# Spreading the first norm with one ones product, and a new order for the first stage, in a one-layer diffusion trunk on one core

## The chip, the core and the metric

The kernel runs on one core of a Trainium2 chip. The core has a matrix engine (TensorE, PE in the profile, with its weight loads listed apart as PEld), VectorE (DVE), ScalarE (ACT), GpSimd (POOL), and queues that issue DMAs (SyncE's is SPq, ScalarE's is ACTq). Each engine runs its own instructions in order and waits on semaphores for the others. The metric is the device time of one execution in microseconds (us), the median of several.

## The reference

One layer of a flow-matching backbone. 1024 latent tokens `x` and 256 context tokens `ctx` of width 1024 go through a feed-forward half step, a token mixing of retention and gated linear attention, and a second feed-forward half step; each is modulated by columns that a condition vector gives. What matters here is the beginning:

```python
cond_lat = jax.nn.silu(c)
m_l = jnp.split(cond_lat @ ada_w[i] + ada_b[i], N_MOD, axis=-1)
x = x + 0.5 * m_l[2][:, None, :] * swiglu(modulate(rms_norm(x, norm1_w[i]), m_l[0], m_l[1]),
                                            ffn1_w1[i], ffn1_w3[i], ffn1_w2[i])

def rms_norm(x, w):
    y = xf * lax.rsqrt(jnp.mean(xf * xf, axis=-1, keepdims=True) + EPS)
def modulate(h, shift, scale):
    return h * (1.0 + scale[:, None, :]) + shift[:, None, :]
def swiglu(h, w1, w3, w2):
    return (jax.nn.silu(h @ w1) * (h @ w3)) @ w2
```

The norm of 1024 tokens needs the sum of squares over the width; scale and shift need products of the condition with 1024 x 1024 blocks of `ada_w`; then come the products with `w1` and `w3`.

## The kernel before

**Layout.** Activations stand with the width on the 128 partitions and tokens along the row: `x` is eight tiles (k = 0 to 7) of 128 x 512 for each of two token groups, 0 and 1. A float product is made of three faster ones: each operand is split in a high part, rounded by ScalarE (`hh`, `wh`, `whi`), and a low part, the rest, made by VectorE (`hl`, `wl`, `wlo`), and TensorE adds up high x high, high x low and low x high. Both parts of four k tiles of one weight chunk come from one 128 x 512 half, `raw`.

**The first stages** (`first1`, L1139 to L1303) do the norm of group 0, its first columns, and the products of six weight chunks i = 0 to 5 (alternating `w1` and `w3`) with the eight k tiles. The order on TensorE, VectorE and ScalarE is the order in which the lines are written, since the call stands in a `manual_schedule` for these three. SyncE's queue follows the order of the text as far as buffers and the limited number of DMAs under way allow.

- `squares` (L547) makes the sum of squares: ScalarE squares a tile, VectorE adds it to `nacc`.
- `rstd_col` (L559) sums `nacc` over the partitions by four products with ones that give columns, and forms power -0.5 of the mean (`pow_half`, L1596): one VectorE step and one on GpSimd. `rows_diag` (L570) multiplies the identity with each column, and `rstd_rows` (L575) spreads the diagonals over all partitions with four more products. The result stands in PSUM (`pr`) and is copied to `rb[0]` (`nrb`).
- A modulation column j (8 and 9 are the scales of k = 0 and 1, 0 and 1 the shifts) can be had in two ways. `pe_load` fetches 512 KB, `pe_sums` (L470) makes partial sums in 16 products on TensorE, ScalarE copies these out of PSUM, `pe_turn` (L481) turns them into a column with a small product, and `pe_out` (L485) adds the bias on ScalarE; `mod_fin` (L526) finishes a scale on VectorE. Or `mod_load` fetches 512 KB and `mod_sum` (L501) sums on VectorE against the condition row that `cond_load` and `cond_silu` (L442, L452) make; scales 10 to 15 go this way.
- The condition's own columns `ccol` come laid out from the host, and `pe_cond` (L457) puts them through Silu.
- `norm_a1` (L599, VectorE) forms the normed and scaled tile, `norm_a2` (L602, ScalarE) adds the shift and rounds it to `hh`, `norm_b` (L605, VectorE) makes `hl`. `norm_a` does the first two.
- `fetch` loads a raw half, `high` and `low` make its two parts, `load` does both. `mms(i, k, js)` issues the products j of weight i with tile k: 0 is high x high, 1 needs `hl`, 2 needs the weight's low part. `warm` issues filler products.

Stage 0 is k = 0, written out by hand (L1190 to L1245). The loop at L1246 has stages st = 1 to 7. In each, behind weight 0's products, come the sums and the scale of tile n = st + 1, and behind weight 2's its shift, `hh` and `hl`, then the second halves of weights (`FIRST`) and the squares of token group 1 (`SQ`, with loads `X1`). Stage 7 has Silu and products of the hidden values, weights 6 and 7 and the second norm instead.

Later phases (the rest of the feed-forward net, the mixing and the second net) use the same primitives; some follow a planner. Between phases the x tiles are read again (L2025).

Of the kernel before, what the change touches and what calls it, by code (L numbers as in the profile page):

```python
# [11 lines left out]
F32 = mybir.dt.float32  # L12
# [378 lines left out]
class Trunk:  # L391
# [36 lines left out]
    def consts(self):  # L428
# [3 lines left out]
        self.pad(cp, 16)  # L432
        self.ident = self.tile(cp, [P, P], F32, "ident")
        nc.scalar.dma_start(self.ident, I["ident"])
# [3 lines left out]
        nc.vector.memset(self.mhalf, -0.5)  # L438
        self.mods = self.tile(cp, [P, 112], F32, "mod")
# [17 lines left out]
    def pe_cond(self, pool):  # L457
        nc = self.nc
        t = self.tile(pool, [P, 36 * KD], F32, "ccol")[:, :33 * KD]
        nc.scalar.dma_start(t, self.I["ccol"])  # L460
        self.sel = t[:, 32 * KD:32 * KD + 2]
        self.ccol = t[:, :32 * KD]
        nc.scalar.activation(self.ccol, self.ccol, AF.Silu)
# [675 lines left out]
    def first1(self, pools, n1):  # L1139
# [28 lines left out]
        def products(i, ks):  # L1168
            for k in ks:
                self.mm3(pss[i], self.wslice(ws[i], k), self.h[0][k], k == 0, k == KD - 1)  # L1170

# [4 lines left out]
        def mms(i, k, js):  # L1176
            w, h = self.wslice(ws[i], k), self.h[0][k]
            for j in js:
                u, v = ((0, 0), (0, 1), (1, 0))[j]
                nc.tensor.matmul(pss[i], w[u], h[v], start=k == 0 and j == 0, stop=k == KD - 1 and j == js[-1])  # L1180
# [7 lines left out]
        x0, x1 = self.x[0], None  # L1188
        self.ndg, idle, pss, acc = 4, self.psA(), {}, None
# [16 lines left out]
        low(0, 0, raw)  # L1206
        self.rstd_rows(n1r, 512, n1, dg=dg, pr=pr)
        raw = high(1, 0)
        self.pe_sums(pc, 0, cur[9])
        warm(WARM[2])  # L1210
        self.norm_a(0, 0, a, b, pr, n1, x0[0])
        rb[0] = self.scr(n1, "nrb")
        nc.scalar.copy(rb[0], pr)
        low(1, 0, raw)
        sm = self.pe_copy(pc, P, n1)
        self.norm_b(0, 0, b, x0[0])
        for i in range(2):
            pss[i] = self.psA()
            mms(i, 0, (0, 2))
        o9 = self.pe_turn(rc, 4, sm[0])  # L1220
        for i in range(2):
            mms(i, 0, (1,))
        load(2, 0)
        self.pe_out(9, o9)
        load(3, 0)
        self.norm_a1(0, 1, a, rb[0], x0[1])
        self.pe_sums(pc, P, cur[1])
        raw = high(4, 0)
        sm = self.tile(n1, [P, P], F32, "csum128", 2)
        nc.scalar.copy(sm, pc[:, P:2 * P])  # L1230
        low(4, 0, raw)
        load(5, 0)
        cur = {}
# [3 lines left out]
        for i in range(2, 6):  # L1237
            if i == 4:
                o1 = self.pe_turn(rc, 6, sm)
                self.pe_out(1, o1)  # L1240
                self.norm_a2(0, 1, b, x0[1])
            pss[i] = (self.psA if i < 4 else self.psB)()
            mms(i, 0, (0, 2, 1))
        self.norm_b(0, 1, b, x0[1])
        self.cond_silu()  # L1245
        for st in range(1, KD):  # L1246
            n = st + 1
            for w in FIRST.get(st, ()):
                fetch(*w)
            if st in X1:  # L1250
                self.load_x(pools, (1,), X1[st])
            if n + 2 < KD:
                cur[10 + n], cur[n + 2] = self.mod_load(10 + n), self.pe_load(n + 2)
# [3 lines left out]
            for i in range(6):  # L1257
                mms(i, st, (0, 2, 1))
                if i == 0 and n < KD:
# [3 lines left out]
                if i == 2 and n < KD:  # L1263
# [7 lines left out]
                if n == KD:  # L1271
# [682 lines left out]
    def run(self):  # L1954
# [18 lines left out]
        warm = self.tile(self.dp, [P, 64], F32, "warm")[:, :8]  # L1973
        nc.scalar.activation(warm, self.mhalf, AF.Silu)
# [48 lines left out]
        for at, (tg, k) in zip(xat, ((tg, 4 * q + k) for tg, q in ((0, 0), (1, 1), (0, 1), (1, 0)) for k in range(4))):  # L2023
            o = TGS[tg][0]
            plan[at].append(lambda tg=tg, k=k, o=o: nc.sync.dma_start(self.x[tg][k], I["xT"][k * P:(k + 1) * P, o:o + 512]))  # L2025
# [204 lines left out]
for _n, _w in (("ada_b", 72), ("norm1_w", 8), ("norm2_w", 8), ("norm3_w", 8), ("final_norm_w", 8),  # L2230
               ("ret_norm_w", 4), ("gla_norm_w", 4), ("gla_b", 4)):
# [9 lines left out]
def layout(inputs):  # L2241
# [3 lines left out]
    A["xT"] = c(g["x"][0].T)  # L2245
# [5 lines left out]
    A["ccol"] = np.zeros((P, 33 * KD), np.float32)  # L2251
    for i, n in enumerate(("c", "c_ctx")):
        A["ccol"][:, i:32 * KD:32] = g[n].reshape(KD, P).T
        A["ccol"][i::32, 32 * KD + i] = 1.0
# [69 lines left out]
```

## Time and profile before

| what | value |
|---|---|
| median of 3 runs | 2091.38 us (2090.43 to 2091.49) |
| the profiled execution's own time | 2092.0 us |
| its span, first to last instruction | 2090.2 us |
| VectorE, ScalarE, GpSimd busy | 70%, 46%, 9% of the span |
| TensorE's granted clock, mean | 0.999 |
| DMA, mean | 175 GB/s |

A row of the timeline gives start, length, engine, line of the code, operation, `out<-in` by tile names, count, and in brackets the idle time of the engine ahead of it with what ended it. A float product on TensorE is two records. Weight loads run beside products.

### The profile page before, as it was taken

What the parts mean: (1) busy time and instruction counts of PE and PEld (TensorE: products, weight loads), DVE (VectorE), ACT (ScalarE), POOL (GpSimd) and SP (SyncE); (2) the same over time, 40 slices, a digit from 0 to 9 for tenths busy, and PEclk for the clock granted to TensorE, in tenths of its full rate; (3) what the DMA queues carried; (4) which work ended last, traced back from release to release, by engine and by line L of the source; (5) the groups of instructions that cost most, each with busy time, mean ns of one, the idle gap of its engine ahead of it and who ended that gap; (6) DMA issues with size and microseconds to landing.
All of it is one profiled execution on the core that took longest, in us unless ns stands there. A gap on an engine that the chain in (4) does not pass through costs nothing.

```text
span 2090.2 us, 34659 instructions
## 1 busy us (share of the span) xinstructions
PE 2075.5 (99%) x12646; PEld 1780.3 (85%) x12646; DVE 1463.5 (70%) x2649; ACT 965.9 (46%) x1806; POOL 198.2 (9%) x196
## 2 busy tenths in 40 slices
PE   9999999999999999999999999999999999999998
PEld 7888888888889999899789988888888888888888
DVE  6889999676775445764687368867776666765676
ACT  5433433435544445564664246444434334334553
POOL 0000000000015664001011001000000000010000
PEclk9999999999999999999999999999999999999999
DMA  9267767459886553673322223342344444477674
GB/s 347 86 236 235 238 219 255 151 168 353 294 290 219 181 185 105 197 217 93 89 76 84 78 75 102 101 161 81 109 159 146 144 164 156 151 240 232 218 228 151
DMA packets 199643, 366.54 MB, mean 175 GB/s; under 512 B 23216, under 2 KB 36400, under 8 KB 199472
## 3 DMA queue, kind: packets, MB, share of 16 engines
q1 hardware_dynamic: 199040, 364.07, 52.4%
q8 instruction: 99, 1.62, 0.3%
q14 instruction: 72, 0.59, 0.1%
q10 hardware_dynamic: 432, 0.26, 0.0%
HBM read 289.66 MB, written 66.19 MB: 170 GB/s over the span
## 4 chain that ended last, share of the span: by engine, by line
PE 89%; DMA 5%; DVE 4%; ACT 1%; issue 1%; SPq 0%; DVEq 0%; POOL 0%; POOLq 0%; ACTq 0%
PE psa L147 17%; PE psa L424 12%; PE psa L426 12%; PE psa L425 12%; PE psb L425 9%; PE psb L426 8%; PE psb L424 8%; PE psb L147 8%; DMA hh<-in_w 1%; DMA raw<-in_w 1%; PE psa L1180 1%; DMA raw<-gd 1%; DVE wlo L420 1%; DVE hl L420 1%; DVE nacc L556 1%
## 5 line engine op out<-in xcount | busy, mean ns | idle before, releaser
L419 ACT ACTIVATE whi<-raw 128x512 fp32r<-128x512 f32 x371 | 233.9, 631 | 498.0 <-issue 160.1
L420 DVE TENSOR_TENSOR wlo<-raw,whi 128x512 fp32r<-128x512 f32 x371 | 254.5, 687 | 176.1 <-ACT whi L419 172.6
L424 PE MATMUL psa<-hh,whi 128*128 128x512 f32 x684 | 266.8, 390 | 0.0
L426 PE MATMUL psa<-hh,wlo 128*128 128x512 f32 x684 | 266.2, 389 | 0.0
L425 PE MATMUL psa<-hl,whi 128*128 128x512 f32 x684 | 266.1, 389 | 0.0
L425 PE MATMUL psb<-hl,whi 128*128 128x512 f32 x568 | 221.3, 390 | 1.0 <-DVE hl L420 0.9
L424 PE MATMUL psb<-hh,whi 128*128 128x512 f32 x568 | 221.1, 389 | 0.0
L426 PE MATMUL psb<-hh,wlo 128*128 128x512 f32 x568 | 221.1, 389 | 0.0
L147 PE MATMUL psa<-hl,whi 128*128 128x512 f32 x384 | 153.1, 399 | 0.0
L147 PE MATMUL psa<-hh,whi 128*128 128x512 f32 x384 | 152.3, 397 | 0.0
L147 PE MATMUL psa<-hh,wlo 128*128 128x512 f32 x384 | 152.0, 396 | 0.0
L424 PEld LDWEIGHTS psa<-hh,whi 128*128 128x128 f32 x684 | 128.4, 188 | 27.2 <-ACT s L693 0.5
L426 PEld LDWEIGHTS psa<-hh,wlo 128*128 128x128 f32 x684 | 128.3, 188 | 26.6 <-DVE wlo L420 0.2
L425 PEld LDWEIGHTS psa<-hl,whi 128*128 128x128 f32 x684 | 128.4, 188 | 26.4
L147 DVE TENSOR_TENSOR wlo<-raw,whi 128x512 fp32r<-128x512 f32 (+1 forms) x132 | 82.8, 643 | 94.0 <-ACT whi L147 90.0
L420 POOL TENSOR_TENSOR hl<-s,hh 128x512 fp32r<-128x512 f32 x88 | 131.8, 1524 | 145.7 <-ACT hh L419 140.5
L147 ACT ACTIVATE whi<-raw 128x512 fp32r<-128x512 f32 (+1 forms) x132 | 77.2, 598 | 119.9 <-PE psa L147 100.6
L425 PEld LDWEIGHTS psb<-hl,whi 128*128 128x128 f32 x568 | 106.6, 188 | 24.3 <-DVE hl L420 2.1
L424 PEld LDWEIGHTS psb<-hh,whi 128*128 128x128 f32 x568 | 106.6, 188 | 22.6 <-ACT hh L419 0.4
L426 PEld LDWEIGHTS psb<-hh,wlo 128*128 128x128 f32 x568 | 106.6, 188 | 22.1 <-DVE wlo L420 0.2
L426 PE MATMUL psa<-hh,hl 128*128 128x256 f32 x392 | 111.1, 283 | 0.0
L424 PE MATMUL psa<-hh,hh 128*128 128x256 f32 x392 | 111.1, 283 | 0.0
(414 smaller groups left out, 4910.9 us busy)
## 6 DMA issues: line engine op xcount, KB each, us to landing
raw<-in_w SPq DMA_DIRECT2D x242, 256.0 KB, 3.3
s<-in_w SPq DMA_DIRECT2D x198, 256.0 KB, 3.9
gd<-s SPq DMA_DIRECT2D x154, 256.0 KB, 2.8
ada<-in_adaT SPq DMA_DIRECT2D x60, 512.0 KB, 4.4
raw<-gd SPq DMA_DIRECT2D x91, 256.0 KB, 3.2
sd<-s SPq DMA_DIRECT2D x44, 256.0 KB, 2.7
raw<-sd SPq DMA_DIRECT2D x44, 256.0 KB, 3.0
hh<-in_w SPq DMA_DIRECT2D x44, 256.0 KB, 4.1
```

The source lines that it names most:

```text
L147: self.rec.add(self.eng, lambda: f(*map(get, a), **{x: get(v) for x, v in k.items()}), outs, ins, name, a, k)
L419: nc.scalar.activation(hi, src, AF.Copy)
L420: (eng or nc.vector).tensor_tensor(out=lo, in0=src, in1=hi.bitcast(F32), op=ALU.subtract)
L424: mm(ps, wa[0], xa[0], start=start, stop=False, skip_group_check=more)
L425: mm(ps, wa[0], xa[1], start=False, stop=False, skip_group_check=more)
L426: mm(ps, wa[1], xa[0], start=False, stop=stop, skip_group_check=more)
L556: nc.vector.tensor_tensor(out=acc[:, :n], in0=acc[:, :n], in1=sq[:, :n], op=ALU.add)
L1180: nc.tensor.matmul(pss[i], w[u], h[v], start=k == 0 and j == 0, stop=k == KD - 1 and j == js[-1])
```

## The change

Eight edits, all but the last two in or for the first stages:

1. The norm of group 0 is spread by one product of ones with the whole of `nacc` (all partitions get the sum), then a logarithm with the bias `eps` and scale 1/D and an exponential with scale -0.5, both on ScalarE, give `rb[0]`. The columns, GpSimd's power, the diagonals and their products go. The table set with both functions is loaded at the start, in place of Silu's.
2. VectorE copies the sums of columns 8, 0 and 9 out of PSUM and puts out these columns (`pe_out` with `dve=True`), ahead of the low parts of weights.
3. The condition's columns come with `cols`, 16 numbers a partition, and Silu is made of an exponential on ScalarE and an add, a reciprocal and a product on VectorE, into a zeroed `ccol`. `ccol`'s own load goes, and the identity's moves from ScalarE's queue to the end of SyncE's first loads. On that queue the halves of weights 2 and 3 move ahead of column 9's load, and those of 4 and 5 ahead of column 1's.
4. Products of stage 0 are in a new order, and column 9's sums come behind the first four of them. Filler products: 30 and 8 for 40, 2 and 4.
5. In stage 1 the scale and shift of tile 2 come behind weights 2 and 3, not 0 and 2. The condition row is loaded behind stage 0's products.
6. The squares of group 1 are spread as 3, 2 and 3 over stages 4 to 6 (were 4, 2, 2), its loads come behind the columns' loads, and in stage 7 its column sum comes behind weight 3.
7. `xT` is stored by the host as two blocks of 1024 x 512, so that a tile is one contiguous piece of memory, here and where x is read again.
8. Padding and constants are moved accordingly.

```diff
-        self.pad(cp, 16)
+        self.pad(cp, 20)
         self.ident = self.tile(cp, [P, P], F32, "ident")
-        nc.scalar.dma_start(self.ident, I["ident"])
+        self.eps = self.tile(cp, [P, 8], F32, "eps")
+        nc.vector.memset(self.eps, EPS)
...
     def pe_cond(self, pool):
         nc = self.nc
-        t = self.tile(pool, [P, 36 * KD], F32, "ccol")[:, :33 * KD]
-        nc.scalar.dma_start(t, self.I["ccol"])
-        self.sel = t[:, 32 * KD:32 * KD + 2]
-        self.ccol = t[:, :32 * KD]
-        nc.scalar.activation(self.ccol, self.ccol, AF.Silu)
+        self.sel = self.col("sel")
+        self.ccol = self.tile(pool, [P, 32 * KD], F32, "ccol")
+        nc.vector.memset(self.ccol, 0.0)
+        e, x = self.tile(pool, [P, 16], F32, "cexp"), self.col("conds")
+        nc.scalar.activation(e, x, AF.Exp, scale=-1.0)
+        nc.vector.tensor_scalar(out=e, in0=e, scalar1=1.0, scalar2=None, op0=ALU.add)
+        nc.vector.reciprocal(e, e)
...
-    def pe_out(self, j, src):
+    def pe_out(self, j, src, dve=False):
+        if dve:
+            self.nc.vector.tensor_scalar(out=self.mods[:, j:j + 73:72], in0=src, scalar1=self.col("ada_b")[:, j:j + 1],
+                                         scalar2=None, op0=ALU.add)
+            return self.mod_fin(j, 0, True)
...
         cur = {j: self.pe_load(j) for j in (8, 0)}
-        n1r = self.rstd_col(self.squares(x0, 512, n1), 512, n1, w=P, ps=rc)
-        fetch(0, 0), fetch(1, 0)
-        cur.update({j: self.pe_load(j) for j in (9, 1)})
-        for i in range(2, 6):
-            fetch(i, 0)
-        self.pe_sums(pc, 0, cur[8]), self.pe_sums(pc, P, cur[0])
-        sm = self.pe_copy(pc, 2 * P, n1)
+        for w in ((0, 0), (1, 0), (2, 0), (3, 0)):
+            fetch(*w)
+        cur[9] = self.pe_load(9)
+        fetch(4, 0), fetch(5, 0)
+        cur[1] = self.pe_load(1)
+        nc.sync.dma_start(self.ident, self.I["ident"])
+        nc.tensor.matmul(pr, self.ones, self.squares(x0, 512, n1), start=True, stop=True)
+        rb[0] = self.scr(n1, "nrb")
+        nc.scalar.activation(rb[0], pr, AF.Ln, bias=self.eps[:, 0:1], scale=1.0 / D)
+        nc.scalar.activation(rb[0], rb[0], AF.Exp, scale=-0.5)
+        sm = []
+        for i, j in enumerate((8, 0)):
+            self.pe_sums(pc, i * P, cur.pop(j))
+            sm.append(self.tile(n1, [P, P], F32, "csum128", 2))
+            nc.vector.tensor_copy(sm[i], pc[:, i * P:(i + 1) * P])
+        o = [self.pe_turn(rc, 2 * i, sm[i]) for i in range(2)]
+        warm(WARM[1])
         raw = high(0, 0)
-        warm(WARM[1])
-        dg = [self.rows_diag(n1r, i, n1) for i in range(4)]
-        o = [self.pe_turn(rc, 2 * i, sm[i]) for i in range(2)]
-        self.pe_out(8, o[0]), self.pe_out(0, o[1])
+        self.pe_out(8, o[0], True)
+        self.norm_a1(0, 0, a, rb[0], x0[0])
+        self.pe_out(0, o[1], True)
+        self.norm_a2(0, 0, b, x0[0])
         low(0, 0, raw)
-        self.rstd_rows(n1r, 512, n1, dg=dg, pr=pr)
+        pss[0], pss[1] = self.psA(), self.psA()
+        mms(0, 0, (0, 2))
         raw = high(1, 0)
...
+        self.norm_b(0, 0, b, x0[0])
         low(1, 0, raw)
...
+        mms(1, 0, (0,)), mms(0, 0, (1,)), mms(1, 0, (1,))
+        raw = high(2, 0)
+        self.pe_sums(pc, 0, cur.pop(9))
+        sm = [self.tile(n1, [P, P], F32, "csum128", 2) for _ in range(2)]
+        low(2, 0, raw)
+        nc.vector.tensor_copy(sm[0], pc[:, :P])
+        raw = high(3, 0)
+        low(3, 0, raw)
+        pss[2], pss[3] = self.psA(), self.psA()
+        mms(2, 0, (0, 1)), mms(1, 0, (2,)), mms(2, 0, (2,)), mms(3, 0, (0, 1))
+        o = self.pe_turn(rc, 4, sm[0])
+        raw = [high(i, 0) for i in (4, 5)]
+        mms(3, 0, (2,))
+        self.pe_out(9, o, True)
         self.norm_a1(0, 1, a, rb[0], x0[1])
-        self.pe_sums(pc, P, cur[1])
...
+        self.pe_sums(pc, P, cur.pop(1))
+        nc.scalar.copy(sm[1], pc[:, P:2 * P])
+        low(4, 0, raw[0])
+        pss[4], pss[5] = self.psB(), self.psB()
+        mms(4, 0, (0, 2, 1))
+        self.pe_out(1, self.pe_turn(rc, 6, sm[1]))
+        self.norm_a2(0, 1, b, x0[1])
+        low(5, 0, raw[1])
+        mms(5, 0, (0, 2, 1))
+        self.norm_b(0, 1, b, x0[1])
         self.cond_load()
...
+            if n + 2 < KD:
+                cur[10 + n], cur[n + 2] = self.mod_load(10 + n), self.pe_load(n + 2)
             if st in X1:
                 self.load_x(pools, (1,), X1[st])
-            if n + 2 < KD:
-                cur[10 + n], cur[n + 2] = self.mod_load(10 + n), self.pe_load(n + 2)
...
-                if i == 0 and n < KD:
+                if i == 2 * (st == 1) and n < KD:
...
-                if i == 2 and n < KD:
+                if i == 2 + (st == 1) and n < KD:
...
-                        r = self.rstd_col(acc, 512, n1)
                         self.c_mul(0, 0, pss[1])
                         self.c_silu(1, 0, pss[2], True)
+                    if i == 3:
+                        r = self.rstd_col(acc, 512, n1)
...
-                src = I["xT"][k * P:(k + 1) * P, o:o + n] if tg < 2 else I["ctxT"][k * P:(k + 1) * P, :]
+                src = I["xT"][tg, k * P:(k + 1) * P] if tg < 2 else I["ctxT"][k * P:(k + 1) * P, :]
...
-        warm = self.tile(self.dp, [P, 64], F32, "warm")[:, :8]
-        nc.scalar.activation(warm, self.mhalf, AF.Silu)
+        nc.scalar.preload_act_table_set("natural_log_exp_and_others")
...
-X1 = {3: range(4), 4: range(4, 6), 5: range(6, 8)}
-SQ = {4: range(4), 5: range(4, 6), 6: range(6, 8)}
-WARM = (40, 2, 4)
+X1 = {3: range(3), 4: range(3, 5), 5: range(5, 8)}
+SQ = {4: range(3), 5: range(3, 5), 6: range(5, 8)}
+WARM = (30, 8)
...
-    A["xT"] = c(g["x"][0].T)
+    A["xT"] = c(g["x"][0].reshape(2, 512, D).transpose(0, 2, 1))
```

More of the change, by code (lines that the diff above doesn't have):

```diff
@@ L1179, in mms @@
                 u, v = ((0, 0), (0, 1), (1, 0))[j]
-                nc.tensor.matmul(pss[i], w[u], h[v], start=k == 0 and j == 0, stop=k == KD - 1 and j == js[-1])
+                nc.tensor.matmul(pss[i], w[u], h[v], start=k == 0 and j == 0, stop=k == KD - 1 and j == 1)
         def sums(j, o):
@@ L1186, in sums @@
             return sm
-        x0, x1 = self.x[0], None
-        self.ndg, idle, pss, acc = 4, self.psA(), {}, None
+        x0, acc = self.x[0], None
+        self.ndg, idle, pss = 4, self.psA(), {}
         rc, pr, pc = self.psB(), self.psB(), self.psB()
@@ L1208, in first1 @@
+        mms(0, 0, (0, 2))
         raw = high(1, 0)
[L1209 to L1213, printed above, removed]
-        low(1, 0, raw)
[L1215 to L1222, printed above, removed]
@@ L2250, in layout @@
     A["adaN"] = c(g["ada_w"][0].reshape(KD, P, 72, P)[:, :, list(PECOL)].transpose(2, 1, 0, 3)).reshape(len(PECOL), P, D)
[L2251 to L2254, printed above, removed]
+    g["conds"] = np.stack([g["c"].reshape(-1), g["c_ctx"].reshape(-1)])
+    g["sel"] = np.stack([np.arange(P) % 32 == i for i in range(2)]).astype(np.float32)
     def cols(v):
```

27 lines of the change are left out of this document (4 added, 23 removed).

## The prediction

> **What bounds the kernel now.** I read the page first, then the windows, then the timeline of the first 62 us, which is the only stretch that the change's own code touches.
>
> ```profile
> span 2090.2 us, 34659 instructions
> PE 2075.5 (99%) x12646; PEld 1780.3 (85%) x12646; DVE 1463.5 (70%) x2649; ACT 965.9 (46%) x1806; POOL 198.2 (9%) x196
> ```
>
> TensorE is busy 2075.5 of 2090.2 us. So VectorE or ScalarE time saved in the middle buys nothing: 14.7 us is all the idle time TensorE has. What can be gained is the time ahead of the first product, and single stalls in the first stages. The windows below are cut at the first product of each stage (a stage is one of the eight k tiles, six groups of three products); the first two are the filler products.
>
> ```profile
> 1.03:4.45 3.42, 3.41 (x16) 3.42 (x17) 0.00 (x0) 1.76 (x3) 0.00 (x0) 1.00 0.72 206
> 4.45:11.86 7.41, 7.41 (x66) 7.21 (x65) 4.23 (x7) 4.90 (x9) 0.00 (x0) 1.00 0.98 357
> 18.45:23.95 5.50, 5.50 (x39) 4.28 (x39) 4.30 (x8) 4.37 (x11) 0.00 (x0) 1.00 1.04 405
> 23.95:29.30 5.35, 5.35 (x38) 3.90 (x36) 3.63 (x7) 2.97 (x7) 0.00 (x0) 1.00 1.01 380
> 29.30:34.42 5.12, 5.12 (x37) 3.90 (x36) 4.05 (x8) 2.27 (x6) 0.00 (x0) 1.00 0.89 316
> 44.68:50.34 5.66, 5.29 (x38) 3.72 (x36) 4.24 (x9) 2.63 (x7) 0.00 (x0) 1.00 1.03 388
> 50.34:55.91 5.57, 5.51 (x37) 4.00 (x38) 4.54 (x8) 2.68 (x7) 0.00 (x0) 1.00 0.47 158
> ```
>
> The columns are the stretch, its length, and busy time of TensorE (with the count of records), of weight loads, VectorE, ScalarE and GpSimd. An undisturbed stage takes 5.12 us (29.30 to 34.42). The stages that begin at 44.68 and 50.34 take 5.66 and 5.57, so 0.54 + 0.45 = 0.99 us is lost there. The rest is ahead of 18.45, and this is its chain:
>
> ```profile
> 1.16 0.45 ACTq L434 DMA_DIRECT2D ident<-in_ident  x1
> 1.71 0.39 ACTq L460 DMA_DIRECT2D ccol<-in_ccol  x1
> 5.68 0.69 DVE L556 TENSOR_TENSOR nacc<-nacc,nsq 128x512 f32<-128x512 f32 x1 [4.68 <-ACT nsq L555]
> 7.11 0.63 ACT L555 ACTIVATE nsq<-x 128x512 f32<-128x512 f32 x1 [1.46 <-DMA x<-in_xT]
> 7.65 0.40 ACT L463 ACTIVATE ccol<-ccol 128x256 f32<-128x256 f32 x1
> 7.77 4.71 DVE L556 TENSOR_TENSOR nacc<-nacc,nsq 128x512 f32<-128x512 f32 x6 [1.40 <-ACT nsq L555]
> 12.54 1.16 PE L565 MATMUL psb<-ones,nacc 128*128 128x128 f32 x8 [0.68 <-DVE nacc L556]
> 13.62 1.08 PE L473 MATMUL psb<-ada,ccol 128*32 128x128 f32 x32
> 13.97 1.01 POOL L1600 TENSOR_TENSOR nr<-nr,mhalf 128x4 f32<-128x4 f32 x1 [13.09 <-DVE nr L1599]
> 15.02 0.87 DVE L572 TENSOR_SCALAR ndiag<-ident,nr 128x128 f32<-128x128 f32 x4 [1.13 <-POOL nr L1600]
> 15.20 0.61 PE L482 MATMUL psb<-ccol,csum 128*128 128x2 f32 x4
> 15.66 1.14 PE L581 MATMUL psb<-ndiag,ones 128*128 128x128 f32 x8
> 16.84 0.75 DVE L595 SCALAR_TENSOR_TENSOR x<-x,mod,psb 128x512 f32<-128x512 f32 x1
> 17.68 0.72 ACT L596 ACTIVATE hh<-x,mod 128x512 fp32r<-128x512 f32 x1 [0.91 <-DVE x L595]
> 18.45 0.50 PE L1180 MATMUL psa<-hh,wh 128*128 128x512 f32 x1
> ```
>
> Read it downwards. The sum of squares grows on VectorE by one add per 4.71/6 = 0.785 us. Its second add comes late, because ScalarE waited 1.46 us for the third x tile; the last add ends at 7.77 + 4.71 = 12.48. Then come the column sums (12.54), the power on GpSimd (13.97), four diagonals on VectorE (15.02), the product that spreads them over the rows (15.66, ends 16.80), the first normed tile (16.84) and its rounding on ScalarE (17.68). From the last add to the first product this is 18.45 - 12.48 = 5.97 us.
>
> **The change part by part: squares.** The two tables that ScalarE's queue loads beside x (64 KB and, by its shape, 128 x 264 x 4 bytes = 132 KB) leave the head, and the 0.40 us Silu at 7.65 with them. Cover is x alone: VectorE's small operations for the condition fall before 5.68, where it waits anyway. If x then keeps up, seven adds run from 5.68 without a gap: 5.68 + 6 x 0.785 + 0.69 = 11.08. If the wait at 7.11 stays, it is 12.48 as now. A gain beyond 11.08 needs the second x tile itself to be earlier; nothing in the trace shows one faster, and I allow 0.7 (10.4). I take 11.08, since the wait is beside the two tables that go. Reading x from a contiguous place I cost at nothing; its effect, if any, is inside these bounds.
>
> **Norm and columns.** The prices of the new steps come from elsewhere in the trace:
>
> ```profile
> 997.16 0.87 ACT L147 ACTIVATE t<-t 128x256 f32<-128x256 f32 x2
> 998.73 1.28 ACT L147 ACT_TABLE_LOAD   x1
> 1000.03 0.60 ACT L147 ACTIVATE sg<-psa 128x512 f32<-128x512 f32 x1
> ...
> 1259.26 0.69 ACT L147 ACTIVATE t<-psb,cols 128x512 f32<-128x512 f32 x1
> 1259.98 0.63 ACT L147 ACTIVATE t<-t 128x512 f32<-128x512 f32 x1
> ...
> L1163 DVE TENSOR_TENSOR wlo<-raw,whi 128x512 fp32r<-128x512 f32 x6 | 4.0, 687 | 0.7 <-ACT whi L1159 0.7
> L572 DVE TENSOR_SCALAR ndiag<-ident,nr 128x128 f32<-128x128 f32 x8 | 1.7, 281 | 1.1 <-POOL nr L1600 1.1
> L1599 DVE TENSOR_SCALAR nr<-psb 128x4 f32<-128x4 f32 x2 | 0.3, 159 | 1.2 <-PE psb L565 1.2
> ...
> ada<-in_adaN SPq DMA_DIRECT2D x9, 512.0 KB, 6.6
> 8.90 1.06 SPq L467 DMA_DIRECT2D ada<-in_adaN  x2
> ```
>
> The two activations at 997.16 are by the code an exponential and a logarithm in place, back to back (0.87 for both), with no table load between, so the pair on the norm needs none. An activation of 128x512 out of PSUM with a column as bias took 0.69 (1259.26), the next one in place 0.63. The one ones product streams the same 512 columns as the four at 15.66: 1.14, of which some 0.93 before TensorE goes on. Counting from the last add at 11.08: product out at 12.25, logarithm to 12.98, exponential to 13.64. Beside it: two groups of column sums at 1.08 / 2 = 0.54 each (12.1 to 13.2); two VectorE copies of 128x128 from PSUM, a form that the trace lacks, bounded by 0.16 (the 128x4 row from PSUM) and 0.28 (the 128x128 row from SBUF), I take 0.22, as PSUM has no slow row here; turns (0.61 / 4 = 0.15 a record); then VectorE adds the bias and forms the scale, 0.16 each by the 128x4 row, instead of ScalarE's step. The scale is there at about 13.86, a little later than the exponential, so the columns and not the norm are now last. First normed tile 13.89 to 14.64, shift column 0.16 to 14.71, ScalarE's 0.72 to 15.47. The eight filler products (16 records at 7.41 / 66 = 0.112, so 1.79) start behind the second turn at 13.78 and end at 15.57; they decide by a hair. First product: 15.57 instead of 18.45, a gain of 2.88; with copies at 0.28 it is 15.63.
>
> **What is late next: stage 0.** Now the same 18 products and their helpers follow a start that is 2.88 earlier, but the relay for the second k tile has not moved as much. TensorE gets the sums of column 9 (0.78 with the gaps around them) behind the first product, where they used to stand ahead of it. I laid the three engines' new orders side by side with the durations above (products 0.2275 apart, 0.75 for a VectorE step of the norm, 0.69 for a weight's low half, 0.72 and 0.63 on ScalarE, 0.04 from one engine to the next). Products of the first four weights run on to 20.4. Then:
> - the low half of weight 4 stands on VectorE behind column 9 and the normed tile 1; column 9 comes out of its turn at 19.2, so that low half ends at 20.97 and TensorE, with (4,0) done at 20.4, waits 0.64 us;
> - ScalarE's high part of tile 1 waits for column 1, which still goes over ScalarE, and ends at 22.80: 0.47 us of wait for stage 1.
>
> Stage 0 so takes 7.28 us where it took 5.50: 1.78 is given back (0.78 moved work, 0.64 + 0.47 of waits, less some 0.1 that the old one lost).
>
> **Stages 1 and 2.** Silu now needs its own table after the logarithm's: 1.28 on ScalarE, behind the rounding of tile 1 and ahead of both condition halves (0.60 each). Behind it stand the copy of column 2's sums and all of tile 2; VectorE's sum for column 10 waits for the second half. The later place of that work in stage 1 covers most of it: tile 2's high part arrives in time, its low part 0.25 late; in stage 1 the low part of tile 1 is 0.34 late. Against 5.35 and 5.12 these stages take 5.44 and 5.35: 0.09 + 0.23 lost. Without the load the model gains 0.12 only.
>
> The Trainium skill (ScalarE: Activation LUTs, What ACT_TABLE_LOAD costs) charges a switch 1.28 for the load and 1.38 more for a drain. The rows at 998.73 and 1000.03 show 1.30 from the load's start to the next Silu, so the trace does not agree; by the page's figure stage 2 would begin some 1.3 us later.
>
> **Loads.** Column 9's 512 KB now stand behind two more weight fetches, 512 KB, 1.3 us at the 405 GB/s of the window at 18.45; the group of these loads lands 6.6 us after issue in the median. Column 9's was issued at 8.90, so lands near 15.5 now; 16.8 then, less 0.5 for the 196 KB that left the head. The sums want it at 16.8: no wait, without much to spare. The identity goes last of them on SP's queue; its next user is the diagonals at 61.08.
>
> **Stages 4 to 7.** These rows say why two stages were long:
>
> ```profile
> 44.99 2.29 DVE L556 TENSOR_TENSOR nacc<-nacc,nsq 128x512 f32<-128x512 f32 x3 [0.29 <-ACT nsq L555]
> 47.20 1.28 DVE L505 CUSTOM_DVE_ANT_0 junk<-ada,condc,cols 128x1024 bf16<-128x1024 f32 x1
> 48.72 0.75 DVE L600 SCALAR_TENSOR_TENSOR x<-x,mod,nrb 128x512 f32<-128x512 f32 x1
> 50.34 0.50 PE L1180 MATMUL psa<-hh,wh 128*128 128x512 f32 x1 [0.37 <-ACT hh L603]
> ...
> 61.08 0.87 DVE L572 TENSOR_SCALAR ndiag<-ident,nr 128x128 f32<-128x128 f32 x4
> 62.38 1.06 PE L581 MATMUL psb<-ndiag,ones 128*128 128x128 f32 x8
> ```
>
> Three adds of x's second half (44.99) hold VectorE until 47.28; behind them are the column (47.20), the normed tile (48.72) and with it the product at 50.34. The change leaves two adds there, 0.785 less. Of the 0.99 lost I take 0.86 back: a low part stays 0.17 late because VectorE runs closer to TensorE than before. The add that is moved lands in stage 6, ahead of the low halves of weight 6, the second norm's column and its diagonals. In the model those end 0.54 after TensorE has come to them (61.06 against 60.5), while the row at 62.38 followed TensorE's own work. Loss 0.50.
>
> **The sum.** 2.88 - 1.78 - 0.09 - 0.23 + 0.86 - 0.50 = 1.1 us. The profiled execution took 2092.0 with its span of 2090.2 and 1.8 around it: 2092.0 - 1.1 = 2090.9. It lay 0.6 above the median of the three runs shown, 2091.4, so on that footing the forecast is 2090.3.
>
> **The rivals.**
> - *Faster: the relay keeps up.* The waits of 0.64, 0.47, 0.34, 0.25 and 0.50 vanish because VectorE's one- and two-element steps take less than 0.16, and x lets the adds end at 10.4: 1.1 + 2.2 + 0.7 = 4.0, so 2087.4. For it: a few tenths per step decide all of them. Against it: five waits must go together.
> - *Slower: x is late all the same.* The ScalarE wait at 7.11 is a straggling DMA and not the two tables. The adds end at 12.48, everything behind moves by 1.4: 1.1 - 1.4 = -0.3, so 2091.7. It decides from an end of the adds at 12.2. For it: the row names the DMA and not a queue; the window to 11.86 moved 357 GB/s, already near 405. Against it: 196 KB less in front.
> - *A pause behind the table load.* If ScalarE needs as long again as the load's own 1.28 before it runs Silu, tile 2 is 1.3 late and stage 2 with it: 1.1 - 1.3 = -0.2, so 2091.6. The rows at 998.73 and 1000.03 speak against it, so it gets little. This is the drain of the Trainium skill's page ScalarE: Activation LUTs, cited above.
> - *The rest moves.* The remaining phases are ordered by a planner, and tiles lie elsewhere in SBUF. TensorE has at most some 10 us of idle time there to win, and a few to lose: I put 2086 or 2096.
> - That the ones product replaces the power but not the wait is in the sum: columns end last, 0.2 us behind the norm.
>
> **How the numbers follow.** Forecast 0.48, faster relay 0.24, late x 0.13, pause 0.04, rest 0.11. No more than 0.2% (4.2 us, about what a measurement can tell from no change) is reached by the forecast, by late x or by the pause. Past it on the fast side are two fifths of the faster rival (0.10, where x is earlier still) and 0.04 of the rest; on the slow side 0.07 of the rest and 0.02 of a late x that also upsets the loads. So faster 0.14, same 0.77, slower 0.09. The forecast's own range is 2089.5 to 2091.5, from an end of the adds between 10.4 and 12.2 and the copies' 0.06; the range 2087.0 to 2092.6 takes in most of the faster rival and both slower ones.
>
> **What would show it.** Right: the last add of the squares near 11.1, the first product near 15.6, a wait of 0.5 us or so for the low half of weight 4, no product stalled by the sixth stage's tile, one table load of 1.28 ahead of the condition's Silu. Wrong: adds that end at 12, a table load between logarithm and exponential, a first product later than 16.5, or a window behind 62 us with idle TensorE that was not there. If the diagonals of the second norm do not hold TensorE, the last term falls.

## The result, and the profile after

| | median | lowest to highest | runs |
|---|---|---|---|
| before | 2091.40 us | 2089.15 to 2094.04 | 19 |
| after | 2094.61 us | 2093.77 to 2096.63 | 19 |

The ratio is 1.0015, with an interval of 1.0009 to 1.0021: the changed kernel is some 3 us slower, above the predicted range of 2087.0 to 2092.6. Its profiled execution took 2094.38 us.

The first lines of the page of after:

```profile
span 2092.5 us, 34600 instructions
PE 2079.1 (99%) x12616; PEld 1775.5 (85%) x12616; DVE 1465.7 (70%) x2655; ACT 967.3 (46%) x1802; POOL 196.8 (9%) x195
```

TensorE has 30 records fewer and is busy 3.6 us longer (2075.5 before). A wait would show as idle time; here work itself must have become slower. Before that question, the first stages, since the change's code is there. The timeline of after, in the columns of the one before:

```profile
8.46 2.28 DVE L565 TENSOR_TENSOR nacc<-nacc,nsq 128x512 f32<-128x512 f32 x3
10.80 1.12 PE L1205 MATMUL psb<-nacc,ones 128*128 128x512 f32 x2 [0.42 <-DVE nacc L565]
11.96 0.69 ACT L1207 ACTIVATE nrb<-psb,eps 128x512 f32<-128x512 f32 x1 [2.14 <-PE psb L1205]
12.57 0.29 DVE L1213 COPY csum<-psb 128x128 f32<-128x128 f32 x1 [1.82 <-PE psb L478]
12.69 0.63 ACT L1208 ACTIVATE nrb<-nrb 128x512 f32<-128x512 f32 x1
12.91 0.64 PE L478 MATMUL psb<-ada,ccol 128*32 128x128 f32 x16 [0.41 <-DVE csum L1213]
13.49 0.87 PE L487 MATMUL psb<-cols,csum 128*128 128x2 f32 x4
14.39 0.22 DVE L492 TENSOR_SCALAR mod<-psb,cols 128x2 f32<-128x2 f32 x1 [0.48 <-PE psb L487]
14.65 0.16 DVE L541 SCALAR_TENSOR_TENSOR mod<-mod,cols 128x1 f32<-128x1 f32 x1
14.92 0.75 DVE L609 SCALAR_TENSOR_TENSOR x<-x,mod,nrb 128x512 f32<-128x512 f32 x1
15.83 0.72 ACT L612 ACTIVATE hh<-x,mod 128x512 fp32r<-128x512 f32 x1 [2.00 <-DVE mod L492]
16.61 0.50 PE L1185 MATMUL psa<-hh,wh 128*128 128x512 f32 x1 [0.36 <-ACT hh L612]
22.32 0.50 PE L1185 MATMUL psb<-hh,s 128*128 128x512 f32 x1 [0.56 <-DVE s L1172]
24.24 1.28 ACT L456 ACT_TABLE_LOAD   x1
24.28 0.50 PE L1185 MATMUL psa<-hh,wh 128*128 128x512 f32 x1 [0.31 <-ACT hh L612]
25.54 1.15 ACT L456 ACTIVATE condc<-condc 128x512 f32<-128x512 f32 x2
62.55 1.13 PE L590 MATMUL psb<-ndiag,ones 128*128 128x128 f32 x8
```

The adds end at 10.74, the norm is spread at 13.32, but the first normed tile waits for its scale until 14.92. One link is new: the sums of column 0 wait 0.41 us for VectorE to copy those of column 8 out of the same PSUM tile. The bias step of column 8 (14.39) then waits for the turns of both columns, which end at 13.49 + 0.87 = 14.36 and share a PSUM tile too; its own turn had ended at 13.87. The first product comes at 16.61. Stage by stage (the same cuts as in the prediction: length, then busy time of TensorE, weight loads, VectorE, ScalarE, GpSimd):

```profile
16.61:24.28 7.67, 6.80 (x55) 4.34 (x55) 5.18 (x11) 3.83 (x9) 0.00 (x0) 1.00 1.03 408
24.28:29.88 5.60, 5.55 (x37) 3.75 (x37) 2.96 (x6) 3.72 (x7) 0.00 (x0) 1.00 0.53 189
29.88:35.47 5.59, 5.54 (x38) 3.99 (x37) 4.67 (x8) 2.89 (x7) 0.00 (x0) 1.00 0.89 300
45.76:50.91 5.15, 5.15 (x38) 3.90 (x36) 4.00 (x7) 2.40 (x7) 0.00 (x0) 1.00 1.01 359
50.91:56.05 5.14, 5.14 (x37) 3.90 (x36) 4.11 (x8) 2.25 (x6) 0.00 (x0) 1.00 0.93 354
```

By 62.55 us all of the early start is used up (62.38 before). So the first stages explain 0.2 us of loss and not 3. The rest is behind them. For each kernel I took the start of the k-th product from the end, and subtracted that of before. This is its lag in us; a positive number is late:

```
at us (before)   106.8  560.4  846.1  994.2 1085.3 1336.0 1662.6 1889.3 2082.9
after             0.57   2.81   0.16  -0.14  -1.60  -1.46   1.15   3.77   2.42
```

The lag grows evenly from 107 to 560 and from 1480 to 1890 us, shrinks from 560 to 850, and drops once at 1020. The groups of products between 1490 and 1935 us show why. Before:

```profile
L424 PE MATMUL psa<-hh,whi 128*128 128x512 f32 x217 | 84.4, 389 | 0.0
L424 PE MATMUL psb<-t2h,whi 128*128 128x512 f32 x40 | 15.6, 389 | 0.0
```

After:

```profile
L424 PE MATMUL psa<-hh,whi 128*128 128x512 f32 x212 | 82.5, 389 | 0.0
L424 PE MATMUL psb<-t2h,whi 128*128 128x512 f32 x40 | 15.8, 395 | 0.0
```

The number behind the bar's comma is the mean of one product in ns. A product of `hh` with a weight takes what it took; one of `t2` with the same weight takes 6 ns more, and so do those of `t1` and `t3`. `hh` and the weights lie at the left end of SBUF, the `t` tiles at the right end. The change has a wider `cols`, a padding of 20 and not 16 numbers and the tile `eps`; in the compiled program this moves every later tile on the left by 128 bytes (`hh00` from 3200 to 3328), while the right end stays. So weights and streamed tile no longer lie a multiple of 256 bytes apart, but 128 beside one. The windows of the same stretch count it: in 445 us before and after do

```profile
1490.00:1935.00 445.00, 444.70 (x1961) 1.00 0.51 170
```

```profile
1490.00:1935.00 445.00, 445.00 (x1943) 1.00 0.50 169
```

products: 18 fewer, 4.1 us of work at 227 ns each.

### The profile page after: what moved, and what is told of

Read it like the earlier page. It is cut to its first block, busy times and chain, and to the rows that moved or that the text cites. A ratio compares the mean times of both kernels' runs of the same rounds, so it can differ in the third digit from the quotient of the medians.

```text
span 2092.5 us, 34600 instructions
## 1 busy us (share of the span) xinstructions
PE 2079.1 (99%) x12616; PEld 1775.5 (85%) x12616; DVE 1465.7 (70%) x2655; ACT 967.3 (46%) x1802; POOL 196.8 (9%) x195
## 4 chain that ended last, share of the span: by engine, by line
PE 96%; DVE 1%; DMA 1%; ACT 1%; issue 0%; SPq 0%; POOL 0%; DVEq 0%; POOLq 0%; ACTq 0%
PE psa L147 18%; PE psa L424 13%; PE psa L426 13%; PE psa L425 13%; PE psb L426 9%; PE psb L425 9%; PE psb L424 9%; PE psb L147 9%; PE psa L1185 1%; PE psb L1185 0%; DVE nacc L565 0%; DMA hl<-gd 0%; PE psb L478 0%; DMA s<-in_w 0%; DVE wlo L420 0%
## 5 line engine op out<-in xcount | busy, mean ns | idle before, releaser
L420 POOL TENSOR_TENSOR hl<-s,hh 128x512 fp32r<-128x512 f32 x88 | 131.7, 1524 | 143.4 <-DMA hl<-sd 81.2
```

Source lines behind the costliest of these rows:

```text
L420: (eng or nc.vector).tensor_tensor(out=lo, in0=src, in1=hi.bitcast(F32), op=ALU.subtract)
```

## The experiments

**Placement alone, both ways.** Three kernels test it. The first is before with its left tiles moved:

```diff
-        self.pad(cp, 16)
+        self.pad(cp, 48)
```

> The kernel before with 128 bytes more of padding ahead of the h tiles and weights (pad of 48 words instead of 16), nothing else. Placement theory (products slow down when the weights, on the left of SBUF, and the tiles that stream, on the right, lie 128 bytes apart modulo 256): products between 1490 and 1750 us go from 227 to some 230 to 233 ns, 256-column products between 560 and 1000 us get about 1 ns faster, and the span is 2.0 to 2.6 us longer than before's. Order theory (the later phases are planned in another order since the first stages changed): no difference within 0.7 us.

It took 2096.66 us, a ratio of 1.0024 (1.0015 to 1.0034), 5 us. The theory holds in kind; its size, 2.0 to 2.6 us, was guessed too low, here and in the next two. The second is the change without the move:

```diff
-        self.pad(cp, 20)
...
-        self.eps = self.tile(cp, [P, 8], F32, "eps")
+        self.eps = self.mhalf[:, 7:8]
```

> The changed kernel with its 128 bytes taken back: no pad behind the columns, and eps kept in a spare column of the tile of minus halves, so h tiles and weights lie where they lay before. Placement theory: the steady 227 ns come back, the span is 2.0 to 2.6 us under the changed kernel's 2092.5, so about equal to before. Order theory: it stays at 2092.5 within 0.7.

2089.80 us, 0.9991 (0.9983 to 1.0): 5 us below the changed kernel by the ratios. The third leaves the left where the change put it and moves the right end as well:

```diff
-        self.pad(edge, 24)
+        self.pad(edge, 56)
```

> The changed kernel with 128 bytes more padding at the right edge (56 words instead of 24), so that the tiles on the right move too and the old distance modulo 256 is restored at new places. If the distance between weights and streamed tiles counts: as with the left part moved back, 2.0 to 2.6 us under the changed kernel. If the place of the weights alone counts (a multiple of 256 being bad): still 230 to 233 ns and no gain. Order theory: no gain.

2090.27 us, 0.9996 (0.9987 to 1.0005), 4 us below the changed kernel. So neither place matters by itself, but the distance between the two. One group between 1490 and 1935 us, in the first kernel, and then in the second, whose line the third has word for word:

```profile
L424 PE MATMUL psb<-t2h,whi 128*128 128x512 f32 x40 | 15.8, 395 | 0.0
```

```profile
L424 PE MATMUL psb<-t2h,whi 128*128 128x512 f32 x40 | 15.6, 389 | 0.0
```

**The products by themselves.** A kernel that does nothing but products, 96 at each distance:

> Leaves the computation out and measures the products by themselves: weights at the left (multiples of 512 bytes), one streamed tile at the right, read from 0, 32, 64, 96, 128, 160, 192 and 224 bytes past a multiple of 256, 96 products at each, first of 512 and then of 256 columns. The whole list runs twice: once with the other engines idle, once while ScalarE copies and VectorE subtracts all the time. Theory A (the two reads of TensorE, weights and streamed columns, get in each other's way by their distance): already in the first pass 512-column products take 226 to 227 ns from start to start at distance 0 and 229 to 233 at distance 128; 256-column products 120.3 at 0 and 119.1 at 128. Theory B (it takes writes of ScalarE or VectorE beside them): the first pass is flat over the distances within 0.5 ns, and only the second shows a difference of 2 to 6 ns. Theory C (neither, but the mixture of weights that change hands in the kernel): both passes flat.

Its windows are cut at the blocks; the second number is the length of 96 products. The first three are 512 columns at distance 0, 64 and 128; then 256 columns at 0, 128 and 192; then the second pass, with VectorE and ScalarE at work, 512 columns at 0 and 128:

```profile
15.59:37.35 21.76, 21.76 (x97) 18.02 (x96) 0.00 (x0) 0.00 (x0) 0.00 (x0) 1.00 0.00 1
...
59.76:81.74 21.98, 21.98 (x97) 18.03 (x96) 0.00 (x0) 0.00 (x0) 0.00 (x0) 1.00 0.00 0
104.15:126.55 22.40, 22.40 (x97) 18.02 (x96) 0.00 (x0) 0.00 (x0) 0.00 (x0) 1.00 0.00 1
193.81:205.32 11.51, 11.51 (x98) 11.50 (x96) 0.00 (x0) 0.00 (x0) 0.00 (x0) 1.00 0.01 1
239.45:250.84 11.39, 11.39 (x98) 11.39 (x97) 0.00 (x0) 0.00 (x0) 0.00 (x0) 1.00 0.01 1
262.11:273.02 10.91, 10.91 (x99) 10.91 (x97) 0.00 (x0) 0.00 (x0) 0.00 (x0) 1.00 0.00 0
291.67:313.43 21.76, 21.76 (x97) 18.02 (x96) 19.95 (x30) 20.54 (x33) 0.00 (x0) 1.00 0.00 1
380.23:402.63 22.40, 22.40 (x97) 18.02 (x96) 21.38 (x31) 21.33 (x34) 0.00 (x0) 1.00 0.00 1
```

Theory A: 21.76/96 = 226.7 ns at distance 0, 22.40/96 = 233.3 at 128, and the same with the other engines busy. The distances 32, 96, 160, 192 and 224 took 233.3 to 234.3, and 64 took 228.9. So the loss needs no other engine: it lies in TensorE's own work and goes by the distance of its two operands. That the two reads hinder each other is the likely reason; no run looks inside. And a length of 256 columns behaves otherwise: 119.9 at 0, 118.6 at 128, 113.6 at 192. That fits the gain of the changed kernel between 560 and 850 us, where the context phase runs products of 256 columns, and it says that a better place than either exists. A second kernel of this kind varied both places:

> Leaves the computation out and measures products alone, 96 of each kind, with the place of the weights (s) and of the streamed tile (m) in bytes past a multiple of 256. Theory: only m - s modulo 256 counts. Then 512 columns take 226.7 ns at (0,0), (0,256), (0,512), (64,64), (128,128) and 233.4 at (0,128), (64,192), (128,0); 256 columns 119.9 at (0,0) and (128,128) and 113.4 at (0,192), (0,448), (0,704), (64,0), (128,64). Rival: the place of one of the two counts by itself, or the distance modulo 512 or more: then the pairs of one distance differ by several ns. For 288 and 128 columns (distances 0, 64, 128, 192) there is no number yet: 288 columns should take 127.5 at the least (288 parts of 113.4 over 256) and 128 columns 56.7, and up to 8 ns more at the distances that disturb.

Rows: 512 columns with (weights, stream) at (128, 128) and (128, 0); 256 columns at (0, 448), (64, 0) and (128, 64):

```profile
103.98:125.78 21.80, 21.80 (x97) 1.00 0.00 1
170.40:192.71 22.31, 22.31 (x97) 1.00 0.00 1
226.63:237.51 10.88, 10.88 (x98) 1.00 0.01 2
248.40:259.71 11.31, 11.31 (x99) 1.00 0.01 1
259.71:270.60 10.89, 10.89 (x99) 1.00 0.00 0
```

For 512 columns the distance modulo 256 is nearly all: 226.7 to 227.2 in the five kinds with 0, 232.3 to 232.4 in the three with 128 (233.3 in the first kernel). For 256 columns there is an exception: (64, 0) has the distance 192 and took 117.8 ns, while (128, 64), also 192, took 113.4. So the distance is not the whole rule, and the rest stays open. Products of 128 columns took 111.7 ns at all four distances, twice the 56.7 that was expected at the least; those of 288 columns took 131.7 to 133.3.

**What the distance is worth in the kernel.** The tiles of the context phase have a pool of their own on the right. A padding above it moves them alone:

```diff
+        self.pad(opn("gap", "right"), 32)
         hc = opn("hc", "right")
...
```

> The kernel of e2 (the change with its left tiles back at their old addresses) with 128 bytes of padding above the tiles of the context phase on the right (hh2, hl2, x2, ghi, glo), so that these alone stand 128 bytes off the left tiles, while the tiles t1, t2, t3 and x stay as they were. Theory of the distance: the 256-column products between 560 and 1000 us, which read one operand on the left and one on the right, start about 1.1 ns sooner after each other (119.1 instead of 120.3 ns), as they did in the changed kernel, and the time is 2.0 us below e2: 2087.6 to 2088.0. Rival (what counts is where the left tiles lie, or the drift has another source): the stretch from 560 to 1000 us is the same as in e2 and so is the time, 2089.8.

2088.37 us, 0.9983 (0.9974 to 0.9991), by the ratios 1.7 us below e2 (the change with its left tiles back) where 2.0 was expected. The two intervals overlap; the traces are clearer: between 650 and 994 us the lag falls by 2.0 us in this kernel and by 0.1 in e2. With 16 numbers in place of 32 the distance is 192 bytes; on before:

> The kernel before, with those 64 bytes of padding above the tiles of the context phase and nothing else. The distance goes from 0 to 192 for about 1730 products (119.9 to 113.4 ns each) and to 64 for 333 (119.9 to 117.8): 11.2 + 0.7, so 11.9 us below before (about 2091.4 to 2092.3): 2079.5 to 2080.5, a ratio of 0.9943, if TensorE stays the bound of that stretch. Rival (another engine or the transfers take its place): 2083 to 2089.

2083.90 us, 0.9965 (0.9952 to 0.9978): 7.3 us less by 64 bytes, where 11.9 was expected: the rival's range, but not for its reason. By the 994th us it is 9.3 ahead of before, 8.7 of that between 560 and 994, and TensorE stayed the bound. But not all products of `hh` and `hl` reached the size of the pure measurement. Two windows of 96 such products each, at the same distance of 192:

```profile
641.29:652.60 11.31, 11.31 (x98) 1.00 0.73 239
716.84:727.72 10.88, 10.88 (x99) 1.00 0.62 196
```

That is 117.8 ns a product in the first and 113.3 in the second. Some 300 of the 1056, nearly all before 700 us, took 117 to 120 ns, and some 740 took 112 to 115. So one distance has two spacings, and 117.8 is also what (64, 0) showed above. What decides between them is open.

**The first stages.** In the changed kernel, the sums of column 0 in a PSUM bank of their own:

```diff
+        p0 = self.psA()
...
-            self.pe_sums(pc, i * P, cur.pop(j))
+            self.pe_sums((pc, p0)[i], i * P, cur.pop(j))
...
```

> The changed kernel with the sums of column 0 in a PSUM bank of their own, so that TensorE need not wait for VectorE's copy of column 8's sums. In the changed kernel TensorE stood 0.41 us at 12.91 for it. If that wait delays the columns: first product 0.8 to 1.1 us earlier than 16.61 (about 15.6, held by the filler products), and the span 0.7 to 1.1 us shorter than 2092.5. If the first product is held by something else, or what follows eats it: under 0.3 us.

The timeline of this kernel:

```profile
11.02 1.12 PE L1206 MATMUL psb<-nacc,ones 128*128 128x512 f32 x2 [0.91 <-DVE nacc L565]
12.54 0.62 PE L478 MATMUL psa<-ada,ccol 128*32 128x128 f32 x16
16.21 0.50 PE L1185 MATMUL psa<-hh,wh 128*128 128x512 f32 x1 [0.36 <-ACT hh L612]
```

From the ones product to the first product it is 5.19 us and not 5.81: the wait for the shared PSUM tile was worth 0.6. The whole took 2095.22 us, 1.002 (1.0011 to 1.0028), beside after's 1.0015, so the runs don't resolve that gain, and the expected 0.7 to 1.1 wasn't seen. With the left tiles back, the two banks, and another order in stage 0 (products with the high halves of weights 4 and 5 ahead of those that need low halves; the turn of column 1 still stands behind three products, but none of them needs a low half now):

> The changed kernel with its left tiles back at their old addresses (as in e2), the sums of column 0 in a PSUM bank of their own (as in e4), and stage 0 in another order: the products with weight 4's high half and weight 5's high half with the high part of x stand ahead of the three products that need low halves, and the turned sums of column 1 come three products earlier. What it tells apart: whether the waits at the head of the first stages (0.56 us for the low half of weight 4, 0.31 us for the high part of tile 1) reach the end. If the chain ahead of the first product and these two waits set the time of the first stages, the head of the second FFN product's rows comes 0.4 us earlier by the bank (as in e4) and 0.5 to 0.9 us earlier by the order, so the time is 0.9 to 1.3 us below e2 (2089.8): 2088.5 to 2088.9. Rival: the stages only trade one wait for another (the relay of mod, high part, product), the gain at the first product is given back by 61 us, and the time is that of e2 within 0.4.

2089.35 us, 0.9987 (0.9978 to 0.9996). Its windows, of stage 0 and of the 18 products around the head of stage 6:

```profile
16.46:23.29 6.83, 6.79 (x54) 1.00 1.03 398
...
49.46:54.87 5.41, 5.41 (x37) 1.00 1.01 385
```

Stage 0 is 0.8 shorter than the 7.67 of after, and 0.27 comes back at stage 6 (the same 18 products took 5.14 in e2). The first product behind the stages starts at 60.44, in e2 at 61.23; so the gain is not given back by then. By the ratios the time is 0.8 below e2, a little less than the 0.9 to 1.3 expected, and the intervals overlap: the trace shows the gain, the times don't resolve it.

**x in two blocks, alone.** Edit 7 on the kernel before:

> The kernel before with edit 7 alone: x is stored by the host as two blocks, so that each x tile is one contiguous piece; its loads are otherwise as they were. Two questions. First, the head: if the contiguous place makes x arrive sooner, the last add of squares ends well before 12.48 us (10.8 to 11.3, as in the changed kernel) and the first product comes at about 17.2 instead of 18.45, with the time 0.5 to 1.2 us below before; if the gain there came from the two tables that left the head, the add ends at 12.0 to 12.9 and the time is that of before within 0.5. Second, a stall of TensorE at 1020 us (1.1 us, for a VectorE tile that waits for ScalarE, which waits 1.9 us for a transfer out of a tile), which the traces of before and of its variants show and those of the changed kernel and of its variants don't: if edit 7 is its cause, ScalarE waits less than 1 us there and TensorE's stall is under 0.3 us, a further 1.2 us; if another part is, the stall is there as before.

2090.77 us, 1.0 (0.9991 to 1.0009), and no gain at the first product (18.45 in before):

```profile
7.22 4.70 DVE L556 TENSOR_TENSOR nacc<-nacc,nsq 128x512 f32<-128x512 f32 x6 [1.33 <-ACT nsq L555]
12.90 1.06 PE L565 MATMUL psb<-ones,nacc 128*128 128x128 f32 x8
18.72 0.50 PE L1180 MATMUL psa<-hh,wh 128*128 128x512 f32 x1
```

The adds end at 11.92, between the two answers that were expected. That is 0.6 sooner than in before, but only 0.1 sooner than in e12, which has x at its old place (12.04; 13.25 in e1), and ScalarE still waits 1.39 us for the third x tile. In the changed kernel and its variants they end at 10.74 to 11.25. So the place of x gave little of the adds' 1.7 us, and the two tables that left the head are the likelier cause; that half was not tried alone. The earlier end did not reach the first product here, because the filler products kept TensorE until 12.90. The stall at 1020 us is there too (ScalarE 1.9, TensorE 1.0 us), as in the timeline of before:

```profile
1019.83 0.51 ACT L147 ACTIVATE t<-t,cT 64x256 f32<-64x256 f32 x1 [1.94 <-DMA s0g<-t]
1021.98 0.41 PE L147 MATMUL psb<-ident,t 128*128 128x128 f32 x2 [1.10 <-DVE t L147]
```

In the timeline of after it is smaller (in e2 ScalarE waits 0.56 us and TensorE not at all):

```profile
1018.20 0.51 ACT L147 ACTIVATE t<-t,cT 64x256 f32<-64x256 f32 x1 [0.82 <-DMA s0g<-t]
```

Between 994 and 1085 us the changed kernel and its variants gain 1.1 to 1.8 us on before, and before's variants -0.8 to 0.4. The instructions there stand in the same order on TensorE, VectorE and ScalarE. What makes the transfer earlier is open.

**Everything that helped.** Two banks and the new stage 0 on e2, with the context tiles at distance 128, and then at 192:

> e5 and e6 in one kernel. If the two gains are independent, as their places in time suggest (before 61 us; 560 to 1000 us), the time is that of e2 less both: 2089.8 - 1.1 - 2.0, so 2086.3 to 2087.1, the fastest of all. If the first stages only trade waits, it is that of e6, 2087.6 to 2088.0; if the distance on the right does nothing, that of e5.

> e10 with 64 bytes of padding above the tiles of the context phase in place of 128, so that a streamed tile there stands 192 bytes past the weights instead of 128. By the measurement of the products alone (e9), a 256-column product takes 113.4 ns at 192, 118.7 at 128 and 119.9 at 0. Between 560 and 1000 us about 1730 products of 256 columns stream a tile of that pool against weights on the left (1056 with hh or hl as both operands, 527 with ghi or glo, 144 with hh or hl against whi), and 333 have the tile as weights (distance 64 then: 117.8). If TensorE stays the bound of that stretch: 1730 times 5.3 plus 333 times 0.1 to 0.9 ns, 9.2 to 9.5 us below e10 (2087.0): 2077.5 to 2078. Rival: something else is close behind there (ScalarE's and VectorE's conversions or the weights' transfers), which takes the place of TensorE: 2081 to 2085.

2087.01 us, 0.9981 (0.9972 to 0.999), and 2080.21 us, 0.9952 (0.9938 to 0.9966). The first lies in the range for two independent gains, but its interval takes in e5 and e6 as well, so the times alone don't show it. The last is the fastest of all, 10 us below before by its ratio; going from 128 to 192 bytes gave 6.1 by the ratios, of the 9.2 expected. The lags of five kernels against before, as above:

```
at us (before)   106.8  560.4  846.1  994.2 1085.3 1336.0 1662.6 1889.3 2082.9
e1 (before+128)   1.05   3.38   1.83   1.34   1.79   1.55   4.14   6.76   6.44
e2 (after back)   0.40   0.15  -0.14  -0.26  -1.68  -1.74  -1.74  -1.74  -2.90
e3 (both moved)   0.73   1.22   0.07  -0.18  -1.94  -1.60  -1.61  -1.61  -1.32
e12 (192 alone)  -0.32  -0.57  -8.44  -9.28  -8.48  -8.64  -8.64  -8.64  -9.46
e11 (all, 192)   -0.67  -0.43  -8.59  -9.12 -10.28 -10.29 -10.29 -10.29 -11.66
```

e1 has the two slopes of after without any of its code; e2 has after's code without the slopes. The step behind 1889 us, from +0.3 in e3 to -1.4 in e11, follows none of the edits and stays open.

## Why the prediction was wrong

The step that failed is the one that costs edit 8, padding and constants, at nothing in the sum, and leaves it to the rival "The rest moves" with a chance of 0.11 and a price of 2096 on its slow side. It rests on the prediction's first sentence, that the change touches the first 62 us only: the 128 bytes move tiles that every later phase reads. Moving the left tiles by 128 bytes costs 1.0015 / 0.9991, 0.24% or 5.0 us, between after and e2. Added to the forecast of 2090.3 this gives 2095.3; 2094.61 was measured. The rival named the mechanism ("tiles lie elsewhere in SBUF") and its price was near, but it was sized from TensorE's idle time. The loss is not idle time: TensorE's busy time grew.

The forecast for the rest, 1.1 us of gain, agrees with what e2 shows as a whole (its interval is 0 to 3.6 us, its middle 1.9), but not by its terms:

| term | predicted | measured (profile of after) |
|---|---|---|
| first product | -2.88 | -1.84 (18.45 to 16.61) |
| stage 0 | +1.78 | +2.17 (7.67 for 5.50) |
| stages 1 and 2 | +0.32 | +0.72 (5.60 + 5.59 for 5.35 + 5.12) |
| the two long stages | -0.86 | -0.94 (5.15 + 5.14 for 5.66 + 5.57) |
| diagonals and the rest, to 62.4 | +0.50 | +0.06 |
| sum there | -1.14 | +0.17 |

- *Squares.* The adds end at 10.74 (11.08 predicted; 10.91 to 11.25 in the variants): right, and with the tables as the likelier reason (e14).
- *Norm and columns.* Logarithm 0.69 and exponential 0.63 as read, without a table load between. The columns end last, as said, but at 14.81 instead of 13.86, although the adds ended 0.34 sooner. Two waits were missing. Column 0's sums write the tile that VectorE is reading and start 0.41 late; the two were costed as if they ran side by side. e4 shows this at 0.6 us. And the bias step of column 8 waits for column 0's turn, some 0.5 us past the end of its own turn; the prediction let it start there. No run takes this wait out. A copy took 0.29 (0.22 taken, 0.28 allowed), the bias step 0.22 (0.16 taken).
- *Stage 0.* The two waits are where they were put: 0.56 (0.64) for the low half of weight 4, 0.31 (0.47) for the high part of tile 1. The stage still took 7.67 and not 7.28, as TensorE's own work in it was 6.80 where the sum has 6.18 (5.50 - 0.10 + 0.78).
- *Stages 1 and 2.* One table load of 1.28 as said, but each stage lost more, 0.25 and 0.47 for 0.09 and 0.23.
- *Table switch.* Silu starts 1.30 us after the load starts (24.24, 25.54), so there is no pause behind it, and that rival is out. The Trainium skill (ScalarE: Activation LUTs, What ACT_TABLE_LOAD costs) would add a drain of 1.38; this trace has no room for it behind the load.
- *Long stages.* Right, in mechanism and size. The diagonals cost less than thought, as the first product behind the stages is late anyway.
- *Not seen at all:* the smaller stall at 1020 us, 1.1 to 1.8 us of gain (1.4 in e2). Without it e2 would be about level with before, so that its total agrees with the forecast is luck.

## What to carry to other kernels

A change of a few bytes in a constant can cost more than the work it comes with saves: compare the tiles' addresses of both kernels, and the mean duration of the same products in both profiles, before looking for waits. Where weights and streamed tiles lie at different ends of SBUF, treat their distance modulo 256 bytes as a parameter, and set it per phase by the number of columns; measure it in the kernel, as the products alone promised 11.9 us and the kernel gave 7.3. A PSUM tile that one engine reads while another is to write its other half was a wait here (0.41 us); give each its own bank where one is free.

## What the runs showed of the hardware

Successive products of 512 columns with a weight load each start 226.7 ns apart when the streamed columns lie a multiple of 256 bytes from the weights, 228.9 at a distance of 64, and 232.3 to 234.3 at the other multiples of 32; products of 256 columns start 119.9 ns apart at distance 0 and 113.4 at 192, where 117.8 was seen too. TensorE's clock was granted at 1.00 in every one of these windows, and VectorE and ScalarE at work beside it changed nothing. The Trainium skill (TensorE: Matmul & The Clock Gate, Step-by-step: what each phase is for) says that TensorE reads weights and streamed columns through two independent ports, so that loading the next weights takes nothing from the running product. The runs do not agree: with products and their weight loads alone at work, the spacing of 512 columns differs by 3% (226.7 to 233.3) with where the two operands lie.
